# Fused matmul, bias and residual on one core: bias row loaded in the weight queue and spread by a late VectorE shuffle, dense dummy products in the head, last tile stored in two pieces

## Chip, cores, metric

One core of one Trainium2 chip. The metric is the device time of one execution in microseconds (us), the median of several runs. The profile's span, which begins at the first instruction it shows, is about 1.8 us shorter than that time.

Names: PE is TensorE, PEld its weight loads, ACT ScalarE, DVE VectorE, POOL GpSimd, SP the engine that issues the transfers. A *tile* is 128 rows of x; there are 64. A *row group* is 8 tiles, loaded and stored together. A *ring* is one of the 16 hardware queues over which the transfers are spread. The *page* is the profiler's summary of one execution. A *dummy* is a product of zeros that nobody reads; it only keeps TensorE busy. The trace also records from when on TensorE had its fast clock: a tile's products of 512 and 256 columns take 0.33 us a pair once the clock is fast.

## The reference

```python
x: [16, 512, 1024]  weight: [1024, 768]  bias: [768]  residual: [16, 512, 768]   # all float32
return (np.matmul(x, weight) + bias + residual).astype(np.float32)
```

That is 62 MB to read and 25 MB to write, and 64 tiles of 128 x 1024 times 1024 x 768.

## The kernel before

Each tile of x is cast to bf16, transposed on TensorE (two bf16 in one fp32 word, `ident` as the other operand), copied out of PSUM by VectorE (`xt`), and multiplied by the bf16 weights in 16 products of 512 and 256 columns. GpSimd adds the bias to the residual; VectorE adds that to the product (`finish`). Three product buffers in PSUM are used in turn, so tile t's products wait for the finish of tile t-3. The first three tiles (the *head*) are multiplied one quarter of W at a time, as W arrives. Everything is issued in a fixed order:

```python
HEAD_ORDER = [('bias',), ('warm', 10), ('cast', 0, 'v'), ('cast', 1, 's'), ('tr', 0), ('tr', 1),
 ('wc', 0, 0, 's'), ('wc', 0, 1, 'v'), ('warm', 4), ('mm', 0, 0), ('mm', 1, 0), ...]
# (kind, row group, first tile, last tile): x loads, W quarters, residual loads, stores
ORDER = [('x', 0, 0, 2), ('w', 0, 0, 2), ('x', 0, 2, 4), ('w', 1, 0, 2), ('w', 2, 0, 2), ('w', 3, 0, 2),
 ('x', 0, 4, 6), ('x', 0, 6, 8), ('r', 0, 0, 5), ('x', 1, 0, 4), ('r', 0, 5, 8), ('r', 1, 0, 5),
 ('x', 1, 4, 8), ('x', 2, 0, 8), ('r', 1, 5, 8), ('r', 2, 0, 8), ..., ('s', 4, 0, 8), ...,
 ('s', 7, 0, 5), ('s', 7, 5, 7), ('s', 7, 7, 8)]
# ... cut ...
    K_(nc.scalar.dma_start(out=bias_row, in_=bias[None, :]))
    for _ in range(WARM):     # dummy products, L191; the ones in the head's gaps are L210
        K_(nc.tensor.matmul(PO[0][:, 0:256], lhsT=warm[:, 0:P], rhs=warm, start=True, stop=True))
    def bias_rows():          # bias to all 128 partitions: ones x bias, then a copy (L196, L200)
        for n0, nl in chunks:
            K_(nc.tensor.matmul(bias_ps[:, n0:n0 + nl], lhsT=ones_row, rhs=bias_row[:, n0:n0 + nl],
                                start=True, stop=True))
        K_(nc.vector.tensor_copy(out=bias_sb, in_=bias_ps))
# ... cut: the head, as HEAD_ORDER says ...
    for t in range(HEAD, n_t):
        cast(t + 2)           # ScalarE
        pool_adds(t + 1)      # GpSimd: residual + bias
        transp(t + 1)         # TensorE, then VectorE's copy to xt
        ...                   # the 16 products of tile t
        finish(t - 1)         # VectorE
```

Of the kernel before, what the change touches and what calls it, by code (L numbers as in the profile page):

```python
# [9 lines left out]
FP32 = mybir.dt.float32  # L10
BF16 = mybir.dt.bfloat16
P = 128
J = 8
X_SLOTS = 2
RO_SLOTS = 4
HEAD = 3
XT_N = 4
XB_N = 4
WARM = 10
EARLY_END = 6  # L20
TMP_SLOT = {0: 3}
ADDS = [6, 0, 7, 8, 1, 9, 2, 10, 3, 11, 4, 12, 5, 13, 14, 15]
HEAD_ORDER = [('bias',), ('warm', 10), ('cast', 0, 'v'), ('cast', 1, 's'), ('tr', 0), ('tr', 1),
 ('wc', 0, 0, 's'), ('wc', 0, 1, 'v'), ('warm', 4), ('mm', 0, 0), ('mm', 1, 0),
 ('cast', 2, 'v'), ('cast', 3, 's'), ('tr', 2), ('tr', 3), ('wc', 1, 0, 's'), ('wc', 1, 1, 'v'),
 ('mm', 2, 0), ('mm', 0, 1), ('mm', 1, 1), ('mm', 2, 1), ('wc', 2, 0, 's'), ('wc', 2, 1, 'v'),
 ('mm', 0, 2), ('mm', 1, 2), ('mm', 2, 2), ('wc', 3, 0, 's'), ('wc', 3, 1, 'v'),
 ('cast', 4, 's'), ('mm', 0, 3), ('mm', 1, 3), ('mm', 2, 3)]
ORDER = [('x', 0, 0, 2), ('w', 0, 0, 2), ('x', 0, 2, 4), ('w', 1, 0, 2), ('w', 2, 0, 2), ('w', 3, 0, 2),
 ('x', 0, 4, 6), ('x', 0, 6, 8), ('r', 0, 0, 5), ('x', 1, 0, 4), ('r', 0, 5, 8), ('r', 1, 0, 5),  # L30
 ('x', 1, 4, 8), ('x', 2, 0, 8), ('r', 1, 5, 8), ('r', 2, 0, 8), ('x', 3, 0, 8), ('s', 0, 0, 8),
 ('r', 3, 0, 8), ('x', 4, 0, 8), ('r', 4, 0, 8), ('s', 1, 0, 8), ('x', 5, 0, 8), ('r', 5, 0, 8),
 ('s', 2, 0, 8), ('x', 6, 0, 8), ('r', 6, 0, 8), ('s', 3, 0, 8), ('x', 7, 0, 8), ('r', 7, 0, 8),
 ('s', 4, 0, 8), ('s', 5, 0, 8), ('s', 6, 0, 8), ('s', 7, 0, 5), ('s', 7, 5, 7),
 ('s', 7, 7, 8)]


@with_exitstack
def kernel(
# [8 lines left out]
    nc = tc.nc  # L48
# [4 lines left out]
    N = weight.shape[1]  # L53
    n_q = K // (2 * P)
    n_t = M // P
    n_s = n_t // J
    chunks = [(0, 512), (512, N - 512)]

    x_d = x2d.rearrange("(S p j) k -> S p j k", p=P, j=J)
    res_d = res2d.rearrange("(S p j) n -> S p j n", p=P, j=J)  # L60
    out_d = out2d.rearrange("(S p j) n -> S p j n", p=P, j=J)
    w_d = weight.rearrange("(q p e) n -> p q e n", p=P, e=2)

    sb = ctx.enter_context(tc.tile_pool(name="sb", bufs=1))
    ps = ctx.enter_context(tc.tile_pool(name="ps", bufs=1, space=bass.MemoryType.PSUM))

    def fixed(pool, name, n, shape, dt):
        return [pool.tile(shape, dt, name=f"{name}", tag=f"{name}{i}", bufs=1) for i in range(n)]

    X = fixed(sb, "x_tile", X_SLOTS, [P, J, K], FP32)  # L70
    R = fixed(sb, "ro", RO_SLOTS, [P, J, N], FP32)
    XB = fixed(sb, "xb", XB_N, [P, K], BF16)
    XT = fixed(sb, "xt", XT_N, [P, n_q, P, 2], BF16)
    PO = fixed(ps, "psum_o", HEAD, [P, N], FP32)
    PT = fixed(ps, "pt", 2, [P, n_q, P], FP32)
    (w_sb,) = fixed(sb, "w_sb", 1, [P, n_q, 2, N], BF16)
    (bias_sb,) = fixed(sb, "bias_sb", 1, [P, N], FP32)
    (bias_row,) = fixed(sb, "bias_row", 1, [1, N], FP32)
    (ones_row,) = fixed(sb, "ones_row", 1, [1, P], FP32)
    (ident,) = fixed(sb, "ident", 1, [P, P], FP32)  # L80
    (warm,) = fixed(sb, "warm", 1, [P, 256], BF16)
    (warm_a,) = fixed(sb, "warm_a", 1, [1, 2], FP32)
    K_ = tc.keep_in_program_order
    w_st = R[1]

    done = set()
    queue = list(ORDER)

    def pump():
        while queue:  # L90
            kind, S, j0, j1 = queue[0]
            if kind == "w":
                need = []
            elif kind == "x":
                need = [("cast", J * (S - X_SLOTS) + j) for j in range(j0, j1)] if S >= X_SLOTS else []
            elif kind == "r":
                need = [("store", S - RO_SLOTS, j) for j in range(j0, j1)] if S >= RO_SLOTS else []
                if S == 1:
                    need = [("wcast", n_q - 1)]
                if S in TMP_SLOT.values():  # L100
                    need = [("add", t) for t in range(EARLY_END) if TMP_SLOT[t // J] == S]
            else:
                need = [("out", J * S + j) for j in range(j0, j1)]
            if not all(n in done for n in need):
                return
            queue.pop(0)
            if kind == "w":
                K_(nc.sync.dma_start(out=w_st[:, 2 * S + j0:2 * S + j1, :], in_=w_d[:, S, j0:j1, :]))
                continue
            if kind == "x":  # L110
                K_(nc.sync.dma_start(out=X[S % X_SLOTS][:, j0:j1, :], in_=x_d[S, :, j0:j1, :]))
            elif kind == "r":
                K_(nc.sync.dma_start(out=R[S % RO_SLOTS][:, j0:j1, :], in_=res_d[S, :, j0:j1, :]))
            else:
                K_(nc.sync.dma_start(out=out_d[S, :, j0:j1, :], in_=R[S % RO_SLOTS][:, j0:j1, :]))
                done.update(("store", S, j) for j in range(j0, j1))
            done.update((kind, J * S + j) for j in range(j0, j1))

    def mark(*what):
        done.add(what)  # L120
        pump()

    def cast(t, how="s"):
        if t < n_t:
            assert ("x", t) in done, t
            src, dst = X[t // J % X_SLOTS][:, t % J, :], XB[t % XB_N]
            if how == "sv":
                K_(nc.scalar.copy(out=dst[:, 0:K // 2], in_=src[:, 0:K // 2]))
                K_(nc.vector.tensor_copy(out=dst[:, K // 2:K], in_=src[:, K // 2:K]))
            else:  # L130
                K_((nc.scalar.copy if how == "s" else nc.vector.tensor_copy)(out=dst, in_=src))  # L131
            mark("cast", t)
# [19 lines left out]
    def row(t, n0=0, nl=N):  # L152
        return R[t // J % RO_SLOTS][:, t % J, n0:n0 + nl]

    def tmp(t):
        return R[TMP_SLOT[t // J]][:, t % J, :]
# [17 lines left out]
    def finish(t):  # L174
        p = PO[t % HEAD]
        if t < EARLY_END:
            K_(nc.vector.tensor_add(out=tmp(t), in0=p, in1=bias_sb))  # L177
            mark("fin", t)
        else:
            assert ("add", t) in done, t  # L180
            K_(nc.vector.tensor_add(out=row(t), in0=p, in1=row(t)))  # L181
            mark("out", t)

    K_(nc.scalar.dma_start(out=bias_row, in_=bias[None, :]))
    K_(nc.vector.memset(warm, 0.0))  # L185
    K_(nc.vector.memset(ones_row, 1.0))
    K_(nc.vector.memset(warm_a, 0.0))
    K_(nc.scalar.copy(out=warm_a, in_=warm_a))  # L188
    make_identity(nc, ident)
    for _ in range(WARM):  # L190
        K_(nc.tensor.matmul(PO[0][:, 0:256], lhsT=warm[:, 0:P], rhs=warm, start=True, stop=True))  # L191

    def bias_rows():
        bias_ps = PO[HEAD - 1]
        for n0, nl in chunks:
            K_(nc.tensor.matmul(  # L196
                bias_ps[:, n0:n0 + nl], lhsT=ones_row, rhs=bias_row[:, n0:n0 + nl],
                start=True, stop=True,
            ))
        K_(nc.vector.tensor_copy(out=bias_sb, in_=bias_ps))  # L200

    pump()
    for kind, *a in HEAD_ORDER:
        if kind == "bias":
            bias_rows()
        elif kind == "cast":
            cast(*a)
        elif kind == "warm":
            for _ in range(a[0]):
                K_(nc.tensor.matmul(PO[1][:, 0:256], lhsT=warm[:, 0:P], rhs=warm, start=True, stop=True))  # L210
        elif kind == "tr":
            transp(a[0])
        elif kind == "wc":
            q, e, eng = a
            copy = {"v": nc.vector.tensor_copy, "s": nc.scalar.copy, "g": nc.gpsimd.tensor_copy}[eng]
            K_(copy(out=w_sb[:, q, e, :], in_=w_st[:, 2 * q + e, :]))  # L216
            if (q, e) == (n_q - 1, 1):
                mark("wcast", q)
        else:
            for e in range(2):  # L220
                for n0, nl in chunks:
                    mm(a[0], n0, nl, a[1], e)
    pump()
    for t in range(HEAD - 1):
        finish(t)
        pool_adds(t)

    for t in range(HEAD, n_t):
# [10 lines left out]
    t = n_t - 1  # L239
    tail = [(PO[t % HEAD], 0, 512), (PO[(t - 2) % HEAD], 512, N - 512)]  # L240
    for p, n0, nl in tail:
        for q in range(n_q):
            for e in range(2):
                K_(nc.tensor.matmul(  # L244
                    p[:, 0:nl], lhsT=XT[t % XT_N][:, q, :, e], rhs=w_sb[:, q, e, n0:n0 + nl],
                    start=(q == 0 and e == 0), stop=(q == n_q - 1 and e == 1),
                ))
        K_(nc.vector.tensor_add(out=row(t, n0, nl), in0=p[:, 0:nl], in1=row(t, n0, nl)))  # L248
    mark("out", t)
    pump()  # L250
    assert not queue, queue
# [30 lines left out]
```

## Time and profile before

211.29 us median of 3 runs (211.27 to 211.53).

| reading | value |
|---|---|
| TensorE busy | 204.3 of 209.6 us |
| one tile in the steady part | 3.04 us of TensorE |
| moved | 87.2 MB, sixteen packets in flight, about 430 GB/s in the steady part |
| tile 3's products start (end of the head) | 21.17 us |
| tile 8: cast ends, transposes start | 32.36, 32.88 us |
| tile 12: cast ends, transposes start | 44.65, 45.03 us |
| last packet of data lands | 208.2 us |

From the page of the kernel before: TensorE's row of part 1, the PE and DMA rows of part 2 (busy tenths in 40 slices of the span), and the chain that ended last.

```profile
PE 204.3 (97%) x1308; PEld 133.6 (64%) x1308; DVE 104.7 (50%) x139; ACT 68.0 (32%) x68; POOL 114.6 (55%) x70
...
PE   7999999999999999999999999999999999999992
...
DMA  6999999999999999999999999999999999999785
...
PE 97%; DVE 1%; issue 0%
```

Both rows are nines nearly throughout. The chain names TensorE alone, but a chain names one engine where two may be equally full.

The head, from the timeline of the kernel before (start us, us, engine, line, operation, out<-in, shape, count; in brackets the idle time before it and what ended it). L131 is the cast, L139 the transposes, L146 the products, L177 a finish.

```profile
3.30 2.92 PE L196 MATMUL psum_o<-bias_row,ones_row 1*128 1x512 f32 x4
...
5.53 1.04 ACT L131 CAST xb<-x_tile 128x1024 bf16<-128x1024 f32 x1 [2.78 <-DMA x_tile<-in_x_dram]
...
6.26 0.96 DVE L200 COPY bias_sb<-psum_o 128x768 f32<-128x768 f32 x1 [5.12 <-PE psum_o L196]
7.13 0.68 DVE L131 CAST xb<-x_tile 128x1024 bf16<-128x1024 f32 x1
...
8.26 1.91 PE L139 MATMUL pt<-ident,xb 128*128 128x128 f32 x8
...
10.82 2.11 PE L146 MATMUL psum_o<-w_sb,xt 128*128 128x512 bf16 x8
...
14.15 6.75 PE L146 MATMUL psum_o<-w_sb,xt 128*128 128x512 bf16 x40 [0.35 <-DVE xt L140]
...
20.73 0.60 PE L139 MATMUL pt<-ident,xb 128*128 128x128 f32 x4
...
21.17 2.76 PE L146 MATMUL psum_o<-w_sb,xt 128*128 128x512 bf16 x16
```

The data of tiles 0 and 1 are there at 5.53 us, when ScalarE casts tile 1. VectorE casts tile 0 only at 7.13, because the copy of the bias stands in front of it, and that copy waited 5.1 us for the bias products.

Further on, the same view, casts and transposes of tiles 8 and 12:

```profile
31.32 3.89 ACT L131 CAST xb<-x_tile 128x1024 bf16<-128x1024 f32 x4 [8.74 <-DMA x_tile<-in_x_dram]
32.88 0.60 PE L139 MATMUL pt<-ident,xb 128*128 128x128 f32 x4
...
43.61 2.94 ACT L131 CAST xb<-x_tile 128x1024 bf16<-128x1024 f32 x3 [8.41 <-DMA x_tile<-in_x_dram]
...
45.03 0.60 PE L139 MATMUL pt<-ident,xb 128*128 128x128 f32 x4
```

ScalarE waited over 8 us for x each time, and a cast takes 1.04 us; so tile 8's cast ends 0.5 us before TensorE wants it, tile 12's 0.4 us before. The transposes show no wait in brackets, and yet there is next to no room.

### The profile page before, as it was taken

The page shows a single profiled execution, that of the slowest core. Times are in us where ns is not written, and L with a number is a line of the kernel's source. Part 1 is how long each engine was busy: PE and PEld are TensorE (multiplying, and loading weights), DVE is VectorE, ACT ScalarE, POOL GpSimd, SP SyncE. Part 2 cuts the span into 40 slices and gives each one's busy share as a digit, 9 for nine tenths or more (in the row PEclk, how much of TensorE's full clock was granted, in tenths as well). Part 3 has the DMA queues.
Part 4 walks back from the last instruction along what each step waited for, and adds up shares of the span by engine and source line. Part 5 has one row for each costly group of instructions (what it writes and reads, how often), then busy time and mean ns, then how long its engine had stood idle before and what let it go on. Part 6 is the DMA issues. An engine that isn't in the chain of part 4 may idle for free.

```text
span 209.6 us, 3135 instructions
## 1 busy us (share of the span) xinstructions
PE 204.3 (97%) x1308; PEld 133.6 (64%) x1308; DVE 104.7 (50%) x139; ACT 68.0 (32%) x68; POOL 114.6 (55%) x70
## 2 busy tenths in 40 slices
PE   7999999999999999999999999999999999999992
PEld 4756666666666666666666666666666666666661
DVE  0473643474375455455544554554455445545542
ACT  2445307060733053323432152330533134321000
POOL 1000099995278980199599702994059910799000
PEclk9999999999999999999999999999999999999999
DMA  6999999999999999999999999999999999999785
GB/s 236 425 434 436 427 403 448 456 406 404 462 450 402 417 441 425 421 458 400 436 458 422 425 403 436 446 441 419 427 427 446 425 413 435 432 419 441 336 379 231
DMA packets 5200, 87.23 MB, mean 416 GB/s; under 512 B 577, under 2 KB 577, under 8 KB 1346
## 3 DMA queue, kind: packets, MB, share of 16 engines
q1 hardware_dynamic: 5184, 87.03, 97.6%
q8 instruction: 10, 0.16, 0.3%
q14 instruction: 4, 0.03, 0.0%
q10 hardware_dynamic: 2, 0.00, 0.0%
HBM read 61.87 MB, written 25.17 MB: 415 GB/s over the span
## 4 chain that ended last, share of the span: by engine, by line
PE 97%; DVE 1%; issue 0%
PE psum_o L146 79%; PE pt L139 14%; PE psum_o L210 1%; PE psum_o L196 1%; PE psum_o L244 1%; PE psum_o L191 1%; DVE xt L140 0%; DVE ro L248 0%; DVE warm L185 0%
## 5 line engine op out<-in xcount | busy, mean ns | idle before, releaser
L146 PE MATMUL psum_o<-w_sb,xt 128*128 128x512 bf16 x1008 | 174.7, 327 | 0.3 <-DVE xt L140 0.3
L146 PEld LDWEIGHTS <-xt 128*128 128x128 bf16 x1008 | 98.8, 98 | 59.1 <-DVE xt L140 0.6
L171 POOL TENSOR_TENSOR ro<-ro,bias_sb 128x768 f32<-128x768 f32 x58 | 103.2, 1818 | 53.5 <-DMA ro<-in_residual_dram 53.5
L131 ACT CAST xb<-x_tile 128x1024 bf16<-128x1024 f32 x62 | 63.2, 1044 | 116.4 <-PE pt L139 58.6
L140 DVE COPY xt<-pt 128x1024 bf16<-128x1024 bf16 x64 | 44.1, 691 | 79.0 <-PE pt L139 78.9
L181 DVE TENSOR_TENSOR ro<-psum_o,ro 128x768 f32<-128x768 f32 x57 | 54.2, 950 | 12.0 <-POOL ro L171 10.9
L139 PE MATMUL pt<-ident,xb 128*128 128x128 f32 x256 | 39.0, 277 | 0.0
L139 PEld LDWEIGHTS pt<-ident,xb 128*128 128x128 f32 x256 | 30.7, 143 | 7.3
L167 POOL TENSOR_TENSOR ro<-ro 128x768 f32<-128x768 f32 x6 | 10.8, 1814 | 25.2 <-DMA ro<-in_residual_dram 25.2
L177 DVE TENSOR_TENSOR ro<-psum_o,bias_sb 128x768 f32<-128x768 f32 x6 | 5.6, 950 | 3.5 <-PE psum_o L146 3.5
L216 ACT CAST w_sb<-ro 128x768 bf16<-128x768 f32 x4 | 3.3, 832 | 3.8 <-DMA ro<-in_weight_dram 3.8
L200 DVE COPY bias_sb<-psum_o 128x768 f32<-128x768 f32 x1 | 1.0, 958 | 5.1 <-PE psum_o L196 5.1
L210 PE MATMUL psum_o<-warm 128*128 128x256 bf16 x14 | 3.4, 416 | 0.0
L191 PE MATMUL psum_o<-warm 128*128 128x256 bf16 x10 | 2.3, 418 | 1.1 <-DVE warm L185 1.1
L196 PE MATMUL psum_o<-bias_row,ones_row 1*128 1x512 f32 (+1 forms) x4 | 2.9, 880 | 0.0
L210 PEld LDWEIGHTS <-warm 128*128 128x128 bf16 x14 | 1.9, 142 | 1.4 <-issue 0.7
L244 PE MATMUL psum_o<-w_sb,xt 128*128 128x512 bf16 (+1 forms) x16 | 2.8, 326 | 0.0
L191 PEld LDWEIGHTS <-warm 128*128 128x128 bf16 x10 | 1.3, 144 | 1.5 <-DVE warm L185 1.1
L244 PEld LDWEIGHTS <-xt 128*128 128x128 bf16 x16 | 1.6, 98 | 1.1
L196 PEld LDWEIGHTS psum_o<-bias_row,ones_row 1*128 1x128 f32 x4 | 1.2, 318 | 1.5 <-issue 1.5
L216 DVE CAST w_sb<-ro 128x768 bf16<-128x768 f32 x4 | 2.0, 553 | 0.0
L188 ACT ACT_TABLE_LOAD x1 | 1.3, 1283 | 1.3 <-PEq L266 1.3
(12 smaller groups left out, 4.0 us busy)
## 6 DMA issues: line engine op xcount, KB each, us to landing
x_tile<-in_x_dram SPq DMA_DIRECT2D x6, 4096.0 KB, 29.8
out_dram<-ro SPq DMA_DIRECT2D x7, 3072.0 KB, 24.7
ro<-in_residual_dram SPq DMA_DIRECT2D x6, 3072.0 KB, 21.3
x_tile<-in_x_dram SPq DMA_DIRECT2D x4, 1024.0 KB, 8.2
x_tile<-in_x_dram SPq DMA_DIRECT2D x2, 2048.0 KB, 25.9
ro<-in_residual_dram SPq DMA_DIRECT2D x2, 1920.0 KB, 22.1
ro<-in_weight_dram SPq DMA_DIRECT2D x4, 768.0 KB, 10.2
ro<-in_residual_dram SPq DMA_DIRECT2D x2, 1152.0 KB, 28.6
```

What stands on the lines that cost most here:

```text
L131: K_((nc.scalar.copy if how == "s" else nc.vector.tensor_copy)(out=dst, in_=src))
L139: K_(nc.tensor.transpose(out=pt[:, q, :], in_=words[:, ts(q, P)], identity=ident))
L140: K_(nc.vector.tensor_copy(out=XT[t % XT_N].rearrange("p q m e -> p (q m e)"), in_=pt.rearrange("p q m -> p (q m)").bitcast(BF16),))
L146: K_(nc.tensor.matmul(PO[t % HEAD][:, n0:n0 + nl], lhsT=XT[t % XT_N][:, q, :, e], rhs=w_sb[:, q, e, n0:n0 + nl], start=(q == 0 and e == 0) ...
L167: K_(nc.gpsimd.tensor_add(out=r, in0=r, in1=tmp(t)))
L171: K_(nc.gpsimd.tensor_add(out=r, in0=r, in1=bias_sb))
L177: K_(nc.vector.tensor_add(out=tmp(t), in0=p, in1=bias_sb))
L181: K_(nc.vector.tensor_add(out=row(t), in0=p, in1=row(t)))
L191: K_(nc.tensor.matmul(PO[0][:, 0:256], lhsT=warm[:, 0:P], rhs=warm, start=True, stop=True))
L196: K_(nc.tensor.matmul(bias_ps[:, n0:n0 + nl], lhsT=ones_row, rhs=bias_row[:, n0:n0 + nl], start=True, stop=True,))
L210: K_(nc.tensor.matmul(PO[1][:, 0:256], lhsT=warm[:, 0:P], rhs=warm, start=True, stop=True))
L244: K_(nc.tensor.matmul(p[:, 0:nl], lhsT=XT[t % XT_N][:, q, :, e], rhs=w_sb[:, q, e, n0:n0 + nl], start=(q == 0 and e == 0), stop=(q == n_q ...
```

## The change

Its intent: take the bias products off TensorE and the bias copy out of VectorE's way in the head (four rows of the bias are loaded in the weight queue and a shuffle spreads them late); keep TensorE's clock high from the start with dense 512-column dummies; let less data follow the last addition.

```diff
-WARM = 10
+WARM = 12
-HEAD_ORDER = [('bias',), ('warm', 10), ('cast', 0, 'v'), ('cast', 1, 's'), ('tr', 0), ('tr', 1),
- ('wc', 0, 0, 's'), ('wc', 0, 1, 'v'), ('warm', 4), ('mm', 0, 0), ('mm', 1, 0),
- ('cast', 2, 'v'), ('cast', 3, 's'), ('tr', 2), ('tr', 3), ...
- ('cast', 4, 's'), ('mm', 0, 3), ('mm', 1, 3), ('mm', 2, 3)]
+HEAD_ORDER = [('cast', 0, 'v'), ('cast', 1, 's'), ('tr', 0), ('tr', 1), ('wc', 0, 0, 's'), ('wc', 0, 1, 'g'),
+ ('warm', 3), ('mm', 0, 0), ('mm', 1, 0), ('cast', 2, 'sv'), ('cast', 3, 'sv'), ('warm', 3),
+ ('tr', 2), ('tr', 3), ...
+ ('bias',), ('cast', 4, 'sv'), ('mm', 0, 3), ('fin', 0), ('mm', 1, 3), ('mm', 2, 3)]
 ORDER: ... ('w', 1, 0, 2), 
+        ('b', 0, 0, 0),
         ('w', 2, 0, 2), ... ('s', 7, 5, 7),
-        ('s', 7, 7, 8)]
+        ('c', 7, 7, 0), ('c', 7, 7, 1)]          # 512 and 256 columns of the last tile
+                K_(nc.sync.dma_start(            # kind "b": partitions 0, 32, 64, 96
+                    out=bias_row.rearrange("(g p) n -> g p n", p=QUAD)[:, 0, :],
+                    in_=bias[None, :].to_broadcast([P // QUAD, N])))
-    K_(nc.scalar.dma_start(out=bias_row, in_=bias[None, :]))
+    K_(nc.gpsimd.memset(bias_row, 0.0))
-        (the ones x bias products and VectorE's copy)
+        K_(nc.vector.stream_shuffle(out=bias_sb, in_=bias_row, mask=[0] * QUAD))
-        K_(nc.tensor.matmul(PO[0][:, 0:256], lhsT=warm[:, 0:P], rhs=warm, start=True, stop=True))
+        K_(nc.tensor.matmul(PO[0][:, 0:512], lhsT=warm[:, 0:P], rhs=warm, start=True, stop=True))
# ... cut ...
```

'sv' halves a cast between ScalarE and VectorE, 'g' is GpSimd, and ('fin', 0) puts tile 0's finish early.

## The prediction

> **What bounds the kernel now.** Two things at once. TensorE: the page gives it 204.3 of 209.6 us; the chain of waits is TensorE throughout; the timeline shows one tile every 3.04 us from 20.7 us on (transposes 0.4, sixteen products 2.6). Transfers: the slices view shows them full from the second slice to the last few, and the packets' times run at about 431 GB/s, sixteen in flight (the Trainium skill, "DMA: Bandwidth & Descriptors", section "Where 436 GB/s comes from", gives 435 as the ceiling; this trace agrees). Following packets end to start, I find at least one of the sixteen rings with no idle time from 1.8 us to the last store: it finishes the store of rows 48-55 at 200.8 us where most finish by 199, then the three last stores at 205.4, 207.2 and 208.2. The others idle 1-3 us around 198-200.
>
> **What the change does, in the head.** Timeline: the ones-times-bias products hold TensorE from 3.30 to 6.2 us; the 0.96 us VectorE copy behind them holds the cast of tile 0 until 7.13, although its data were there at 5.5 (ScalarE's cast of tile 1 began at 5.53). Without them tile 0 is cast at 5.5-6.2, transposed from about 6.3 (before: 8.26), and the first real products start at about 8.4 (10.82), when W0's halves are cast (ScalarE 7.4-8.24; the GpSimd half about 8.6, guessed). Dense 512-column dummies should bring the fast clock by 5-8 us; before, 256-column dummies still followed each other every 0.23 us at 8 us and the fast pace appears at about 12. (The Trainium skill, "TensorE: Matmul & The Clock Gate", Part 1: about 3.4 us of sustained activity lifts the half clock.) W1 to W3 still land at 11.8, 13.6, 15.5. The head's products end at about 18.7 (20.73). The shuffle, estimated 0.9 us (like the 0.96 us copy), and x's third piece (18.1) put the first finish at about 18.4-19.4, so tile 3's products start near 19.5 instead of 21.17: 1.6 us gained locally.
>
> **Why little is left.** x rows 8-11 land at 30.8 and their first cast ends at 32.36; the transposes of tile 8 start at 32.88: only 0.5 us slack. Tile 12's data land at 43.1, its cast ends at 44.65, its transposes start at 45.03: 0.35 us slack. The transfers are back to back from 1.75 us and don't move. So TensorE waits about 1.2 us before tile 8 and 0.1 before tile 12, and keeps about 0.3 us. Later slacks (tile 16: 2.8; buffers freed by finishes: 1.5 or more) don't bind.
>
> **Tail.** The last store's packets ran 207.1-208.2, directly behind the store before it, so cutting it in two removes almost no ring time. The never-idle ring doesn't profit from an earlier TensorE either. Bias in the load queue costs four 3 KB rows, about 0.12 us on some rings. Expected in total: 0 to 0.4 us.
>
> **Predicted** 211.1 us, range 210.5 to 211.6 (8 in 10); faster by over 2%: 0.01, within 2%: 0.98, slower: 0.01.
>
> **What would show it.** Right: first real product near 8.4 us, tile 3's products near 19.5, a TensorE wait of about 1 us on ScalarE's cast before tile 8, transposes of tile 12 not before about 44.7, last packets at about 208 us. Wrong: tile 8 transposed near 31.3 with no wait, or last packets before 207.5.
>
> **What would make it wrong.** Loads landing earlier (the bias no longer competes at the start) would move everything; a slow GpSimd cast (over 2 us) or a slow shuffle would eat the head's gain; if the slow ring is an accident of this run, the tail gives 0.5 us more.

## The result, and the profile after

211.33 us median (211.25 to 211.64, 4 runs) against 211.41 (211.27 to 211.58, 4 runs) of the kernel before. The ratio is 0.9999, 95% interval 0.9981 to 1.0016: the same. A ratio here is always the mean time of one kernel's runs over that of the other's of the same rounds, so not quite the ratio of the medians quoted.

From the page of the changed kernel, TensorE's row of part 1 and the two lines of the chain that ended last:

```profile
PE 202.7 (97%) x1298; PEld 130.2 (62%) x1298; DVE 104.7 (50%) x140; ACT 67.7 (32%) x69; POOL 116.0 (55%) x72
...
PE 83%; DMA 14%; ACT 1%; SPq 0%; DVE 0%; issue 0%; ACTq 0%
PE psum_o L161 69%; DMA x_tile<-in_x_dram 14%; PE pt L154 12%; PE psum_o L255 1%; ACT xb L146 1%; DVE ro L259 0%; SPq L116 0%; SPq L119 0%; ACTq L146 0%
```

The span is 209.6 us as before, but the chain now runs through a load of x for 14% of it. The head, from the timeline of the changed kernel (L154 the transposes, L161 the products, L208 the shuffle, L192 a finish, L143/L144/L146 the casts):

```profile
5.56 0.69 DVE L146 CAST xb<-x_tile 128x1024 bf16<-128x1024 f32 x1 [4.43 <-DMA x_tile<-in_x_dram]
...
6.40 1.32 PE L154 MATMUL pt<-ident,xb 128*128 128x128 f32 x8
...
8.31 1.46 PE L161 MATMUL psum_o<-w_sb,xt 128*128 128x512 bf16 x8
...
12.03 6.75 PE L161 MATMUL psum_o<-w_sb,xt 128*128 128x512 bf16 x40 [0.27 <-DVE xt L155]
...
16.12 1.01 DVE L208 STREAM_SHUFFLE bias_sb<-bias_row 128x768 f32<-128x768 f32 x1
18.19 0.43 DVE L144 CAST xb<-x_tile 128x512 bf16<-128x512 f32 x1 [1.06 <-DMA x_tile<-in_x_dram]
...
18.54 1.82 DVE L192 TENSOR_TENSOR ro<-psum_o,bias_sb 128x768 f32<-128x768 f32 x2
...
18.88 0.66 PE L154 MATMUL pt<-ident,xb 128*128 128x128 f32 x4
...
19.54 2.76 PE L161 MATMUL psum_o<-w_sb,xt 128*128 128x512 bf16 x16
```

Tile 0 is cast at 5.56 instead of 7.13 us, the first products start at 8.31 instead of 10.82, and tile 3's products start at 19.54 instead of 21.17: 1.63 us gained here. The same places as before at tiles 8 and 12:

```profile
31.65 3.89 ACT L146 CAST xb<-x_tile 128x1024 bf16<-128x1024 f32 x4 [8.98 <-DMA x_tile<-in_x_dram]
32.75 0.66 PE L154 MATMUL pt<-ident,xb 128*128 128x128 f32 x4 [1.34 <-ACT xb L146]
...
43.92 2.94 ACT L146 CAST xb<-x_tile 128x1024 bf16<-128x1024 f32 x3 [8.39 <-DMA x_tile<-in_x_dram]
45.02 0.66 PE L154 MATMUL pt<-ident,xb 128*128 128x128 f32 x4
```

TensorE now waits 1.34 us for tile 8's cast, and tile 12's transposes start at 45.02 us against 45.03 before. The gain is gone by then, and TensorE runs to the end as it did.

The last stores, kernel before and then the changed one, from the list of DMA issues (count, KB each, us from issue to landing; the third number was not resolved for one of them):

```profile
out_dram<-ro SPq DMA_DIRECT2D x1, 384.0 KB, 2.3
```

```profile
out_dram<-ro SPq DMA_DIRECT2D x1, 256.0 KB
out_dram<-ro SPq DMA_DIRECT2D x1, 128.0 KB, 2.3
```

The piece that follows the last addition is a third of what it was and takes the same 2.3 us. Its last packet lands at 208.18 us, before at 208.22.

### The profile page after: what moved, and what is told of

Its sections match the earlier page's. It is cut to its first block, busy times and chain, and to the rows that moved or that the text cites. A ratio compares the mean times of both kernels' runs of the same rounds, so it can differ in the third digit from the quotient of the medians.

```text
span 209.6 us, 3119 instructions
## 1 busy us (share of the span) xinstructions
PE 202.7 (97%) x1298; PEld 130.2 (62%) x1298; DVE 104.7 (50%) x140; ACT 67.7 (32%) x69; POOL 116.0 (55%) x72
## 4 chain that ended last, share of the span: by engine, by line
PE 83%; DMA 14%; ACT 1%; SPq 0%; DVE 0%; issue 0%; ACTq 0%
PE psum_o L161 69%; DMA x_tile<-in_x_dram 14%; PE pt L154 12%; PE psum_o L255 1%; ACT xb L146 1%; DVE ro L259 0%; SPq L116 0%; SPq L119 0%; ACTq L146 0%
## 5 line engine op out<-in xcount | busy, mean ns | idle before, releaser
L161 PE MATMUL psum_o<-w_sb,xt 128*128 128x512 bf16 x1008 | 174.0, 326 | 0.3 <-DVE xt L155 0.3
L161 PEld LDWEIGHTS <-xt 128*128 128x128 bf16 x1008 | 98.5, 98 | 59.0 <-DVE xt L155 0.7
L146 ACT CAST xb<-x_tile 128x1024 bf16<-128x1024 f32 x60 | 61.3, 1044 | 113.9 <-PE pt L154 60.1
L154 PE MATMUL pt<-ident,xb 128*128 128x128 f32 x256 | 38.7, 275 | 1.6 <-ACT xb L146 1.3
L154 PEld LDWEIGHTS pt<-ident,xb 128*128 128x128 f32 x256 | 29.9, 142 | 10.8 <-ACT xb L146 2.0
L205 PE MATMUL psum_o<-warm 128*128 128x512 bf16 x12 | 5.3, 632 | 1.2 <-DVE warm_a L201 1.2
L192 DVE TENSOR_TENSOR ro<-psum_o,bias_sb 128x768 f32<-128x768 f32 x6 | 5.6, 949 | 0.0
L205 PEld LDWEIGHTS <-warm 128*128 128x128 bf16 x12 | 1.7, 145 | 3.9 <-issue 2.7
L226 POOL CAST w_sb<-ro 128x768 bf16<-128x768 f32 x1 | 0.8, 823 | 5.5 <-DMA ro<-in_weight_dram 5.5
L146 DVE CAST xb<-x_tile 128x1024 bf16<-128x1024 f32 x1 | 0.7, 694 | 4.4 <-DMA x_tile<-in_x_dram 4.4
L143 ACT CAST xb<-x_tile 128x512 bf16<-128x512 f32 x3 | 1.8, 616 | 3.4 <-PE psum_o L161 1.7
L144 DVE CAST xb<-x_tile 128x512 bf16<-128x512 f32 x3 | 1.2, 424 | 2.4 <-DMA x_tile<-in_x_dram 2.4
L220 PE MATMUL psum_o<-warm 128*128 128x512 bf16 x6 | 1.6, 379 | 0.0
L259 DVE TENSOR_TENSOR ro<-psum_o,ro 128x512 f32<-128x512 f32 (+1 forms) x2 | 1.1, 558 | 0.9 <-PE psum_o L255 0.8
```

The lines of the kernel that those rows point to most:

```text
L143: K_(nc.scalar.copy(out=dst[:, 0:K // 2], in_=src[:, 0:K // 2]))
L146: K_((nc.scalar.copy if how == "s" else nc.vector.tensor_copy)(out=dst, in_=src))
L154: K_(nc.tensor.transpose(out=pt[:, q, :], in_=words[:, ts(q, P)], identity=ident))
L161: K_(nc.tensor.matmul(PO[t % HEAD][:, n0:n0 + nl], lhsT=XT[t % XT_N][:, q, :, e], rhs=w_sb[:, q, e, n0:n0 + nl], start=(q == 0 and e == 0) ...
L192: K_(nc.vector.tensor_add(out=tmp(t), in0=p, in1=bias_sb))
L205: K_(nc.tensor.matmul(PO[0][:, 0:512], lhsT=warm[:, 0:P], rhs=warm, start=True, stop=True))
```

## The experiments

The theory has two limits. First, x for tiles 8 and 12 lands when it lands, and takes the head's gain away. Second, even if it didn't, the transfers themselves end at about 208 us, because at least one ring has no idle time. The rival is that the late x is the whole story, so that mending it brings 1.6 us.

Leaving out the store of row group 4 is the tool against the second limit: 3.1 MB less to move, some 7 us of transfers, without touching any engine's work. Its rows stay unwritten, so these runs are wrong (relative error NaN). Two finer load orders are the tool against the first. The kernel before ran too: medians 211.57, 211.54 and 211.40 us, each on another chip.

### Finer loads (e1_after_finer)

```diff
- ('r', 0, 0, 5), ('x', 1, 0, 4), ('r', 0, 5, 8), ('r', 1, 0, 5), ('x', 1, 4, 8),
+ ('r', 0, 0, 2), ('r', 0, 2, 5), ('x', 1, 0, 2), ('r', 0, 5, 8), ('x', 1, 2, 4), ('r', 1, 0, 2),
+ ('x', 1, 4, 6), ('r', 1, 2, 5), ('x', 1, 6, 8),
```

> The changed kernel with its loads of rows 0-15 cut finer and reordered (same bytes), so that x for tiles 8 and 12 lands 2.5 to 5 us earlier. Theory (two limits: late x in the head, the transfers themselves at the end): no TensorE wait before tile 8, tile 12's transposes near 43.5 us instead of 45.02, the last product near 204.2 instead of 205.75, but the last packets still at about 208 us, because the rings have the same bytes and no idle time; time 211.0 to 211.4, ratio to before 0.998 to 1.000. Rival (the late x was the only thing that took the head's gain): time about 209.7, ratio about 0.9925.

Measured: correct, 211.66 us (211.35 to 212.04, 6 runs), ratio 1.0005 (0.9993 to 1.0017), just above the range of the theory and far from the rival's. Tile 12's transposes start at 43.33 us as expected, but the last product starts at 204.96 instead of the 203.8 that keeping the gain would give, because of a wait I had not expected. It is the only wait of TensorE between 20 and 70 us, from the waits of that run (who waited for what: us in total, times, longest):

```profile
PE psum_o L161 <- DVE xt L155: 1.1, 1, 1.1
```

Followed back in its timeline: tile 16's products wait for VectorE's copy; that copy stands behind the finish of tile 13; that waits for GpSimd's addition, and that for the residual of tiles 13 to 15. So there was a third cap in the load order. The run is no clean test of the second limit: about 0.5 us of TensorE's gain was left, and none came out at the end.

### The changed kernel without that store (e3_after_skip)

```diff
- ('s', 4, 0, 8), ('s', 5, 0, 8),
+ ('s', 5, 0, 8),
```

> The changed kernel without the store of row group 4 (3.1 MB, about 7 us of transfer; wrong result on purpose), so that the transfers have slack at the end. TensorE is untouched by it: tile 8 still waits about 1.3 us, last product at 205.75. Theory: then the end follows TensorE, and only the split of the last store can show: last packets at 207.7 to 208.0, time 210.9 to 211.3. Rival (transfers alone limit everything): the time falls by several us, to 205 or less.

Measured: 211.48 us (211.35 to 211.50, 5 runs), ratio 0.9992 (0.9980 to 1.0005); last packet at 208.25 us. Both lie a little above the ranges I gave; the rival (several us) is out. With 3.1 MB less to move the time does not fall: here TensorE, held by the late x, sets the end.

### Both (e4_finer_skip)

Both edits above together.

> Both of the above: the finer loads and no store of row group 4 (wrong result on purpose). Theory: both limits are lifted, so the head's 1.5 us comes through to the end: last product near 204.2, last packets near 206.4, time 209.4 to 209.9, ratio to before 0.991 to 0.9935, and 1.4 us or more faster than the finer loads alone. Rival (late x alone): the same time as the finer loads alone, both near 209.7.

Measured: 210.73 us (210.59 to 210.80, 5 runs), ratio 0.9958 (0.9946 to 0.9970); last product 204.82 us. It is 0.93 us faster than the finer loads alone, so the transfers do hold those back; but the whole gain does not come through, for the reason found above (its largest wait of TensorE in the steady part is again on `xt`). The number expected was a miss, the direction not.

### The kernel before without that store (e5_before_skip)

> The kernel before without the store of row group 4 (wrong result on purpose): the control for the two runs above. Theory: TensorE's order and the last store's issue at about 206.2 us stay, so the time stays within 0.2 us of before (211.1 to 211.4), 0 to 0.2 us slower than the changed kernel without that store (the split's worth). Rival (transfers alone limit the kernel before): several us faster.

Measured: 211.40 us (211.25 to 211.47, 5 runs), ratio 0.9990 (0.9978 to 1.0002). The time is as expected, but it is not slower than the changed kernel without that store (211.48), so no worth of the split shows in the times of this pair (the traces show 0.1 us, see the tail below). In this run the head happened to be 0.36 us shorter than in the profile of before (tile 4's transposes at 20.37 instead of 20.73), and tile 12 still came no earlier than 44.97, behind a cast that started at 43.87: the late x already caps the kernel before when its head is short.

### Finer loads, third cap removed (e6_after_finer2)

```diff
- ('x', 2, 0, 8), ('r', 1, 5, 8),
+ ('x', 2, 0, 4), ('r', 1, 5, 8), ('x', 2, 4, 8),
```

on top of the finer loads. (The text counts one tile too far: the products that waited were tile 16's, behind tile 17's transposes.)

> The finer loads again, and in addition the residual of tiles 13-15 moved ahead of half of x for tiles 16-23, because the first finer order still lost 1.1 us at tile 17 (VectorE's finish of tile 13 waited for that residual). Theory: no TensorE wait over 0.4 us after tile 3, last product near 204.1 us, but the transfers end the run: last packets 207.7 to 208.6, time 211.1 to 211.7, ratio to before 0.998 to 1.001. Rival (TensorE's order alone sets the time once it keeps the 1.6 us): ratio about 0.992.

Measured: correct, 211.73 us (211.55 to 212.03, 5 runs), ratio 1.0005 (0.9992 to 1.0019). TensorE has no wait over 0.3 us after the first dummy; its last product starts at 203.80 us, against 205.48 in the changed kernel. The two additions that follow it, from the timelines of the changed kernel (first fence) and of this run (second):

```profile
204.98 1.23 DVE L259 TENSOR_TENSOR ro<-psum_o,ro 128x512 f32<-128x512 f32 x2 [0.77 <-PE psum_o L255]
```

```profile
203.31 1.23 DVE L259 TENSOR_TENSOR ro<-psum_o,ro 128x512 f32<-128x512 f32 x2 [0.77 <-PE psum_o L255]
```

All of the head's 1.6 us reaches the end of TensorE's work, and the time does not move.

### The same without that store (e7_finer2_skip, and again as e12_finer2_skip_again)

> The same without the store of row group 4 (wrong result on purpose), so that the transfers have slack at the end. Theory: the head's whole gain of about 1.6 us comes through: last product near 204.1, ratio to before 0.991 to 0.993, 1.3 us or more faster than the run with that store. Rival: the same as the run with that store, or, if another wait takes the gain, about 0.996 as with the first finer order.

> The changed kernel with finer loads and without the store of row group 4 once more (wrong result on purpose), on this chip, as the pair for the run without dummies: 209.5 to 209.8, ratio to before 0.990 to 0.993.

Measured: 209.57 us (209.54 to 209.69, 4 runs), ratio 0.9908 (0.9895 to 0.9922); on another chip 209.76 us, ratio 0.9918 (0.9904 to 0.9931). That is 2.16 us below the run with the store, by the medians, though both end TensorE's work within 0.2 us of each other. From the list of DMA issues, the last two stores with all stores (first fence) and without one (second):

```profile
out_dram<-ro SPq DMA_DIRECT2D x1, 256.0 KB, 4.5
out_dram<-ro SPq DMA_DIRECT2D x1, 128.0 KB, 4.3
```

```profile
out_dram<-ro SPq DMA_DIRECT2D x1, 256.0 KB, 2.5
out_dram<-ro SPq DMA_DIRECT2D x1, 128.0 KB, 2.3
```

With all stores, the last piece takes 4.3 us to land instead of 2.3: it is issued 1.7 us earlier than in the changed kernel (at 204.57 instead of 206.24) and then queues. That is where the head's gain goes once the load order lets it through. Counting packets in the trace of the run with all stores, a mean of 9.0 are in flight between 206 and 207 us, 2.0 between 207 and 208, and 1.1 from there to the last packet at 208.54: most rings have finished, and one or two stragglers set the end.

### The last store whole again (e8_finer2_skip_whole)

```diff
- ('c', 7, 7, 0), ('c', 7, 7, 1)]
+ ('s', 7, 7, 8)]
```

> The same without that store, and with the last tile's store whole as before: the split by itself, where the transfers have slack. Theory: the split is worth 0.1 to 0.4 us here, because only 128 KB instead of 384 KB follow the last addition; so 0.1 to 0.4 us longer than the split form. Rival (the split is worth nothing anywhere, or costs): 0 or less.

Measured: 209.68 us (209.60 to 209.74, 4 runs), ratio 0.9912, against 0.9908 for the split form: 0.11 us by the medians, with overlapping intervals. The times alone thus don't show a worth of the split. The traces do: from the start of the last product to the last packet it is 2.79 us here, and 2.70 in the split form (2.68 in its second run). So the split is worth about 0.1 us where the transfers have slack, the low end of what was expected. The 384 KB take 2.3 us from issue to landing, as the 128 KB of the split form do: between these two the landing time hardly depends on the size.

### The kernel before in the same surroundings (e9_before_finer2_skip)

> The kernel before with the finer loads and without the store of row group 4 (wrong result on purpose): the control. Theory: its TensorE order never met the late x, so lifting both limits gives it only 0 to 0.3 us: ratio 0.998 to 1.000, last product near 205.6, and 1.3 to 1.9 us slower than the changed kernel in the same surroundings; that difference is the change's own worth. Rival (the finer loads themselves make the gain): it gains about as much as the changed kernel does.

Measured: 210.93 us (210.45 to 211.00, 5 runs), ratio 0.9965 (0.9953 to 0.9978); last product at 204.80 us. The kernel before gains 0.6 us, more than I allowed, and the change's own worth is 1.36 us by the medians. Its profiled run had a shorter head: tile 3's products at 20.55 us instead of 21.17. The three profiles of the kernel before agree with a head that varies with the clock: the later the trace's record has the fast clock (9.35 us here, 11.22 in e5, 12.12 in the profile of before), the later tile 3's products start (20.55, 20.80, 21.17). The late x had hidden the short heads, as e5 showed.

### No dummies (e10_finer2_skip_nodummy)

```diff
-WARM = 12
+WARM = 0
```

and both `('warm', 3)` taken out of the head, on e7.

> The changed kernel in the surroundings where its gain shows (finer loads, no store of row group 4, wrong result on purpose), without any dummy products: the bias part alone. Theory: the dummies only bring the fast clock forward; without them it should come about 3 to 7 us after the first transposes at 6.4 us, that is at 9 to 13 us instead of 5.4 to 6, the first real products run at half pace, and 0.4 to 1.5 us of the head's gain goes: time 210.0 to 211.1. Rival (the bias part is the whole gain, because the head waits for W's loads anyway): within 0.15 us of the run with dummies.

Measured: 209.69 us (209.65 to 209.81, 5 runs), ratio 0.9916 (0.9902 to 0.9929), against 209.76 and 0.9918 for the form with dummies. My theory fell, the rival stands: the dummies are worth nothing here. (What remains, the bias off TensorE, the halved casts, GpSimd's half of W and the early finish, was not taken apart by any run.) The timeline of the run without them says why:

```profile
6.35 1.94 PE L154 MATMUL pt<-ident,xb 128*128 128x128 f32 x8 [6.35 <-DVE xb L146]
...
8.28 2.72 PE L161 MATMUL psum_o<-w_sb,xt 128*128 128x512 bf16 x8
...
12.29 6.75 PE L161 MATMUL psum_o<-w_sb,xt 128*128 128x512 bf16 x40 [0.35 <-DVE xt L155]
...
18.22 0.43 DVE L144 CAST xb<-x_tile 128x512 bf16<-128x512 f32 x1 [1.03 <-DMA x_tile<-in_x_dram]
...
19.57 2.76 PE L161 MATMUL psum_o<-w_sb,xt 128*128 128x512 bf16 x16
```

Here the clock is slow until 11.03 us by the trace's record: the first eight products take 2.72 us where the changed kernel needs 1.46. But the next step waits for x and W anyway. The head's 40 products start only 0.26 us later than in the changed kernel, and tile 3's products 0.03 us later, because those wait for the finish of tile 0, which stands on VectorE behind the half cast that x's third piece releases at 18.2 us in both.

### A try at the end of the transfers (e11_finer2_shed)

```diff
- ('s', 7, 0, 5),
+ ('s', 7, 0, 5, 120),      # partitions 0-119, then 120-127
```

> A try at the transfers' end, correct result: the finer loads with all stores, and rows 56-60's store cut into partitions 0-119 and 120-127, which by the skill's rule go over 15 and 8 rings instead of 16, so that the 16th ring carries 120 KB less and eight others 15 KB more. If the slowest ring is the 16th: last packets 0.3 to 1.5 us earlier than the 208.5 of the uncut form, time under 211.4. If it is one of the first eight: about 0.5 us later. Else: the same within 0.2 us. No theory of the change hangs on it; it asks whether the slowest ring can be relieved.

Measured: correct, 216.37 us (215.98 to 217.02, 4 runs), ratio 1.0235. It is 4.6 us slower than the uncut form (211.73) and 5 us slower than before, which none of the cases I had listed covers. From the view by stages (stretch in us, its length, busy us of PE, PEld, DVE, ACT, POOL, clock, DMA share, GB/s), the stretch in which that store runs, uncut (e6) and cut:

```profile
200.00:205.00 5.00, 4.08 (x26) 2.25 (x24) 2.54 (x4) 0.00 (x0) 0.00 (x0) 1.00 0.94 398
```

```profile
200.00:205.00 5.00, 4.00 (x25) 2.19 (x23) 2.46 (x4) 0.00 (x0) 0.00 (x0) 1.00 0.96 249
```

The transfers are as busy (0.96 against 0.94) and move 249 instead of 398 GB/s; the trace has the packets of 15,360 bytes at a median of 1,072 ns instead of 573. The rule I had relied on is in the Trainium skill, "DMA: Bandwidth & Descriptors", section "Why a DMA increments its semaphore by 16 and not by 1": a transfer uses the largest number of engines up to 16 that divides its outer dimension, 15 for 120 partitions. This run fits that (about 15 packets in flight instead of 16). Why each packet takes nearly twice as long stays open. A candidate is "SBUF — State Buffer", section "Door 1: The DMA port swizzle", by which eight partitions in a fixed pattern share a port; a division by 15 would break that pattern and let two rings meet at one port. No run tests it. Which ring is the slowest stays open too.

What the two-by-two says, in medians (us):

| loads and kernel | all stores | without row group 4's store |
|---|---|---|
| as they were, kernel before | 211.57 | 211.40 |
| as they were, changed kernel | 211.33 (before in its own call 211.41) | 211.48 |
| finest, changed kernel | 211.73 | 209.57 |
| finest, kernel before | not run | 210.93 |

For the changed kernel, lifting one limit alone brings nothing; lifting both brings about 1.9 us (ratio to before 0.9908 instead of 0.9999). No correct version beat either kernel: the two with finer loads are level with them. One rival is not closed: the transfers' own end at 208.5 us was seen only with the finer loads. The times of their packets, summed and divided by 16, are 204.9 us against 204.6 in the kernel before, so the finer cutting itself may account for some 0.3 us of that end; no run has TensorE early enough to show the end of the loads as they were.

## Why the prediction was right

- **The time.** 211.1 predicted, 211.33 measured; the range held it, and "within 2%" was right.
- **The head.** Right, nearly to the tenth: first transposes at 6.40 (6.3), first products at 8.31 (8.4), tile 3's products at 19.54 (19.5), 1.63 us gained locally (1.6). There is luck in the last: the profile of before that both figures start from has the longest head of three. Against the heads of e5 and e9 (20.80 and 20.55) the gain is 1.3 and 1.0 us. The shuffle took 1.01 us (0.9). GpSimd's half of W was done by 8.27 us, better than guessed.
- **The dummies.** Half right. The fast clock came at 6.95 us by the trace's record (5 to 8 predicted). But I listed it among the sources of the gain, and the run without dummies shows that it is none: x's third piece and VectorE's order end the head.
- **Tiles 8 and 12.** The mechanism was right: a 1.34 us wait at tile 8 (1.2). The kept gain was mis-sized: 0.3 us predicted, 0.01 us measured, since the cast of tile 12 began 0.3 us later than in the profile of before (43.92 against 43.61). The cause is not the bias rows in the queue, or not they alone: the kernel before without a store (e5), which has no such rows in that queue, has 43.87. So the step that was off is that the transfers "don't move": over the four profiles with the loads as they were this cast starts at 43.61 to 44.02 us, a spread as large as the gain that was to be kept.
- **"Later slacks (tile 16: 2.8; buffers freed by finishes: 1.5 or more) don't bind."** This step was wrong, though it cost nothing in the predicted kernel. I had looked at the finishes' ends, not at what stands behind them on VectorE. In the profile of before, the copy for tile 16 ends at 59.48 us and its products start at 60.65: 1.17 us of slack, less than the 1.6 at stake. The first finer load order ran into it and lost 1.1 us.
- **The tail.** The number was right: the last packet lands at 208.18 us (208.22 before). The reason given, the ring without idle time, was not what set it in these two kernels: from the start of the last product to the last packet it is 2.79 us before and 2.70 in the changed kernel, the same as without a store (2.79 in e5, 2.68 in e3), so there the end follows TensorE, less 0.1 us for the split. It is 3.8 and 4.7 us only in e1 and e6, where TensorE ends earlier and all stores run. That an earlier TensorE does not then move the transfers' end is shown, for the finest loads, by the pair with and without the store (e6 and e7): 2.16 us between them at the same end of TensorE's work. That it is a single ring without idle time is inferred: the trace does not name the ring of a packet, and I joined packets end to start. The packet counts at the end agree with one or two stragglers.

## What to carry to other kernels

When an engine is busy 97% of the time, look whether the transfers are as full before you shorten the engine's work: a gain in one of two full resources is returned at the next point where they meet, here 12 us after it was made. To see such a point in advance, list for each load the gap between the end of what it releases and the start of what needs that; the smallest gap downstream, counted along in-order engines too, is all that an earlier start can keep. To prove it, lift one limit at a time and then both; an experiment that lifts only one may show nothing and mislead.

## What the Trainium skill lacked or had wrong

- "DMA: Bandwidth & Descriptors", on how many engines a transfer uses: it does not say what a division other than by 16 costs in rate. Here 120 of 128 partitions went at 249 GB/s in the stretch where the uncut store went at 398, and the time rose from 211.73 to 216.37 us.
- "Runtime: NRT & Kernel Launch", section "Instruction fetch mechanics", calls the cost of crossing a 16 KiB block of instructions mostly hidden. It gives no time that a block takes from the transfers of data. The profiles of both kernels list ten such transfers (0.16 MB in all), each of 0.95 to 1.10 us, and during nine of them 15 instead of 16 packets of data are in flight. No run tests what they cost in time.
- "TensorE: Matmul & The Clock Gate", Part 1, gives about 3.4 us of sustained activity before the fast clock, and a transition around 4 us that varies by 0.5 us from run to run. Here it varied more: in nine profiled runs with dense dummies from 1.2 us on it came at 4.9 to 7.0 us, that is after 3.8 to 5.8 us. In the three profiles of the kernel before it came at 9.4 to 12.1 us; there one-row fp32 products stand between the dummies, and these are of 256 columns. What such thin products count for is not on the page, and no run here isolates them.
